# First pieces of a decoder layer in three transfers, and the last LayerNorm's mean from row sums of the last weights

## The chip, the cores and the metric

The kernel runs on one NeuronCore of a Trainium2 chip. The metric is the device time of one execution in microseconds. The times of several executions are given as a median with the lowest and the highest; one more execution was taken by the hardware profiler, and its trace is what the views below show. TensorE (PE) multiplies, VectorE (DVE), ScalarE (ACT) and GpSimd (POOL) work on elements, SyncE (SP) issues most of the transfers.

## The reference

One decoder layer for one sequence of 256 tokens, width 1024, all in float32:

```python
proj  = x @ w_in                      # [q | k | v | B | C | h | gate_attn | gate_conv]
y_att = attention(rope(q), rope(k), v) @ w_attn_out      # 8 heads of 64, causal
y_cnv = (B * causal_dwconv3(C * h)) @ w_conv_out
mix   = (sigmoid(g_att + b) * y_att + sigmoid(g_cnv + b) * y_cnv) @ w_o
x     = layer_norm(alpha * x + mix, ln1_g, ln1_b)
u     = causal_dwconv3(x @ w_up)                         # 2 x 2816 columns
f     = (silu(u_gate) * u_val) @ w_down                  # 2816 -> 1024
x     = layer_norm(alpha * x + f, ln2_g, ln2_b)          # eps 1e-5
```

`alpha` is 2 to the power 1/4. The last line, over rows of 1024, is the part whose end is changed.

## The kernel before, in words

Every product is made in three matmuls: an operand a is split into a high part (a copy rounded by the type fp32r) and a low part (a minus the high part), and high x high, high x low and low x high are added in PSUM. ScalarE makes the high part (`split_h`, L192, or `hl_split`, L219), VectorE the low part (`split_l`, L197, or L220). So each weight passes once through ScalarE and once through VectorE before TensorE reads it.

The weights (and x transposed) lie packed in device memory as chunks of up to 128 x 2048 numbers. `issue_dma` sends one chunk at a time on SyncE's queue into one of three `raw` buffers; `PIECES` says where a chunk is cut into several transfers. Chunk k of the first eight holds 128 rows of x transposed (256 columns), then those rows of the weights of q (512), k (512) and v (512).

The head of the program: the pieces of chunk 0 and 1 are issued; `warm_up` runs small matmuls on a tile `zeros` that VectorE has just set; VectorE casts x's first piece (L574) and makes its low part (L575), casts q's weights (L577) and makes their low part (L579); TensorE then runs q's passes on chunk 0 (`qkv_passes`, L568: pass 0 is high x high, pass 2 uses the low part of x, pass 1 the low part of the weights), and k's and v's behind it as their pieces land (ScalarE casts those, L219). Chunks 1 to 7 follow in a loop. Afterwards come convolution, gates and attention products, the mixing product, the first norm and the feed-forward part, in an order written out by hand; `slot` splits each weight unit a few units ahead of its use.

In the feed-forward part the 22 row blocks `f_tile(i)` of the hidden activations are made one after another and multiplied with the rows of `w_down` (`down`, `mm3`, L305 to L307) into four PSUM banks `dacc[t][nh]`: t is the block of 128 tokens, nh the half of 512 columns. The last `TAIL` = 8 rows of blocks are done for token block 0 first, then for token block 1 in three parts: half 0 of the columns with all eight (24 matmuls of 512), then columns 512 to 768 (`e2`) and columns 768 to 1024 (`e3`), 24 matmuls of 256 each (`down_part`). While TensorE does block 1, VectorE and GpSimd finish block 0: `residual` (L779, L781: alpha times x plus the bank, and `bn_stats`), `norm_stats` (L757 `bn_aggr` on VectorE, L758 the power -0.5 on GpSimd), `norm_apply` (L762 and L763 on VectorE for each half), and the output transfers.

Block 1's end, `finish(1)`: the residuals of the first three quarters are added as they come; behind the last matmul stand L1012 (add e3), L1013 (`bn_stats`), L757, L769 (subtract the mean and multiply by the gain, two halves), L758 beside it, and L766 (multiply by the power and add the bias) in pieces of 640 and 384 columns, each followed by its output transfer (on SyncE's and on ScalarE's queue).

Of the kernel before, what the change touches and what calls it, by code (L numbers as in the profile page):

```python
# [8 lines left out]
F32 = mybir.dt.float32  # L9
F32R = mybir.dt.float32r  # L10
# [3 lines left out]
ALU = mybir.AluOpType  # L14
# [123 lines left out]
def layer_kernel(ctx: ExitStack, tc: tile.TileContext, x, wpack, cpack, ln1_g, ln1_b, ln2_g, ln2_b, out):  # L138
# [11 lines left out]
    def acc_bank(name):  # L150
        return psum.tile([P, 512], F32, tag="acc", name=name)
# [4 lines left out]
    def scratch(shape, name, bufs=None, tag="scr"):  # L156
        return tmp.tile(shape, F32, tag=tag, name=name, bufs=bufs or 6)
# [11 lines left out]
    def issue_dma(c):  # L169
        while len(raws) <= c and len(raws) < len(chunks):  # L170
# [5 lines left out]
            if i == XR_CHUNK:  # L176
                nc.sync.dma_start(xr, x[0].rearrange("(t p) d -> p t d", p=P))

    def alloc(u, part, tag):
        k, n = units[u]["shape"]  # L180
        units[u][part] = wp.tile([P, k, n], F32R, tag=tag, name=f"{tag}{u}", bufs=HL_BUFS)
# [6 lines left out]
    def split_h(u):  # L188

        issue_dma(units[u]["chunk"] + RAW_BUFS - 1)  # L190
        alloc(u, "h", "wh")
        nc.scalar.activation(units[u]["h"], raw_of(u), AF.Copy)  # L192

    def split_l(u):

# [28 lines left out]
    nc.vector.memset(zeros, 0.0)  # L224
# [5 lines left out]
    warm = ps_bank("warm")  # L230

    def warm_up(n):
        for i in range(n):
            nc.tensor.matmul(warm[:, 0:P], zeros, zeros, start=True, stop=True)

    warm_up(36)

    mask = cst.tile([P, 384], F32, name="mask")
    nc.gpsimd.memset(mask, 0.0)
# [6 lines left out]
    neghalf = cst.tile([P, 1], F32, name="neghalf")  # L246
    nc.gpsimd.memset(neghalf, -0.5)
    neghalf2 = cst.tile([P, 1], F32, name="neghalf2")
    invf = cst.tile([P, 8], F32, name="invf")
    for i, f in enumerate(INV_FREQ):  # L250
        nc.gpsimd.memset(invf[:, i:i + 1], f)
# [312 lines left out]
    def qkv_passes(k, m, ts, ps):  # L564
        wh, wl = qkv_weights(k, m)
        for t in ts:
            for p in ps:
                nc.tensor.matmul(banks[m][t], (xl if p == 2 else xh)[:, k, t * P:(t + 1) * P], wl if p == 1 else wh,  # L568
                                 start=k == 0 and p == 0, stop=k == KT - 1 and p == 2)
# [1 line left out]

    split_start(1)
    issue_dma(RAW_BUFS - 1)
    nc.vector.tensor_copy(xh[:, 0, :], raws[0][:, 0:S])  # L574
    nc.vector.tensor_tensor(xl[:, 0, :], raws[0][:, 0:S], xh[:, 0, :].bitcast(F32), op=ALU.subtract)  # L575
    w0, wh0, wl0 = raw_of(1), units[1]["h"], units[1]["l"]
    nc.vector.tensor_copy(wh0[:, 0], w0[:, 0])  # L577
    qkv_passes(0, 0, (0, 1), (0, 2))
    nc.vector.tensor_tensor(wl0[:, 0], w0[:, 0], wh0[:, 0].bitcast(F32), op=ALU.subtract)  # L579
    qkv_passes(0, 0, (0, 1), (1,))  # L580
    split_part(1, 1, 2)
# [116 lines left out]
    def ps_pair(name):  # L698
        return pairs.tile([P, 2, 512], F32, tag="pair", name=name)
# [54 lines left out]
    def norm_stats(r, stats, pieces):  # L754

        mv = tmp.tile([P, 4], F32, tag="mv", name="mv", bufs=4)
        nc.vector.bn_aggr(mv[:, 0:2], stats[:, 0:pieces, :])  # L757
        nc.gpsimd.tensor_tensor(mv[:, 3:4], mv[:, 1:2], neghalf, op=ALU.pow)  # L758
        return mv

    def norm_apply(o, r, mv, g, b):
        nc.vector.scalar_tensor_tensor(o, r, mv[:, 0:1], g, op0=ALU.subtract, op1=ALU.mult)  # L762
        nc.vector.scalar_tensor_tensor(o, o, mv[:, 3:4], b, op0=ALU.mult, op1=ALU.add)  # L763

    def norm_second(r, mv, ln, cs):
        nc.vector.scalar_tensor_tensor(r[:, cs], r[:, cs], mv[:, 3:4], ln[:, 1, cs], op0=ALU.mult, op1=ALU.add)  # L766

    def norm_first(r, mv, ln, cs):
        nc.vector.scalar_tensor_tensor(r[:, cs], r[:, cs], mv[:, 0:1], ln[:, 0, cs], op0=ALU.subtract, op1=ALU.mult)  # L769
# [8 lines left out]
    def residual(t, nh, bank, res, r, stats, piece, c0, c1):  # L778
        nc.vector.scalar_tensor_tensor(r[:, c0:c1], res[:, t, c0:c1], ALPHA, bank[:, c0 - nh * 512:c1 - nh * 512],  # L779
                                       op0=ALU.mult, op1=ALU.add)  # L780
        nc.vector.bn_stats(stats[:, piece, :], r[:, c0:c1])  # L781
        if piece == 0:
            with_eps(stats)
# [19 lines left out]
        residual(0, nh, banks[nh], xr, r1[0], st1[0], nh, nh * 512, nh * 512 + 512)  # L803
    norm1(0, r1[0], st1[0])
    nc.scalar.activation(neghalf2, neghalf, AF.Silu)
    banks = [acc_bank(f"o1{nh}") for nh in range(2)]
    for k in range(4):
        wo_rows(k, 1, banks)
# [106 lines left out]
    def down(i, ts=(0, 1), nhs=(0, 1)):  # L915
        un = units[U[("dn", i // 2)] + i % 2]
        ft = f_tile(i)
        for t in ts:
            for nh in nhs:
                mm3(dacc[t][nh], ft[:, 0, t * P:(t + 1) * P], ft[:, 1, t * P:(t + 1) * P],  # L920
                    un["h"][:, 0, nh * 512:(nh + 1) * 512], un["l"][:, 0, nh * 512:(nh + 1) * 512],
                    i == 0, i == NP - 1 or (t == 1 and nh == 1 and i == NP - TAIL - 1))

    def down_part(i, bank, c):
        un = units[U[("dn", i // 2)] + i % 2]
        ft = f_tile(i)
        mm3(bank[:, 0:256], ft[:, 0, P:2 * P], ft[:, 1, P:2 * P],
            un["h"][:, 0, c * 256:(c + 1) * 256], un["l"][:, 0, c * 256:(c + 1) * 256], i == NP - TAIL, i == NP - 1)
# [4 lines left out]
    def take(n):  # L933
        out = []
        for stage, i in list(pending):
            if len(out) < n and i not in [p for _, p in out]:
                out.append((stage, i))
                pending.remove((stage, i))
        return out
# [49 lines left out]
        slot(k, stages)  # L989


    def finish(t):
        r = x1[:, t]
        stats = tmp.tile([P, 4, 6], F32, tag="stats", name=f"rstats{t}", bufs=2)
        if t == 0:
            for k in range(TAIL):
                down(NP - TAIL + k, (t,))
                slot(tail_from + k, take(2))
            assert not pending
            for nh in range(2):  # L1000
                residual(t, nh, dacc[t][nh], x1, r, stats, nh, nh * 512, nh * 512 + 512)
        else:
            for i in range(NP - TAIL, NP):
                down(i, (t,), (0,))
            nc.vector.scalar_tensor_tensor(r[:, 512:1024], x1[:, t, 512:1024], ALPHA, dacc[t][1], op0=ALU.mult, op1=ALU.add)
            for c in range(2):
                residual(t, 0, dacc[t][0], x1, r, stats, c, c * 256, c * 256 + 256)
            for c in range(2, 4):
                bank = ps_pair(f"e{c}")[:, 0]
                for i in range(NP - TAIL, NP):  # L1010
                    down_part(i, bank, c)
                nc.vector.tensor_tensor(r[:, c * 256:c * 256 + 256], r[:, c * 256:c * 256 + 256], bank[:, 0:256], op=ALU.add)  # L1012
                nc.vector.bn_stats(stats[:, c, :], r[:, c * 256:c * 256 + 256])  # L1013
        mv = norm_stats(r, stats, 2 if t == 0 else 4)
        if t == 0:
            for c in range(2):
                cc = slice(c * 512, (c + 1) * 512)
                norm_apply(r[:, cc], r[:, cc], mv, ln2[:, 0, cc], ln2[:, 1, cc])
                nc.sync.dma_start(out[0, t * P:(t + 1) * P, cc], r[:, cc])
            return  # L1020
        for c in range(2):
            norm_first(r, mv, ln2, slice(c * 512, c * 512 + 512))
        for cc, queue in ((slice(0, 640), nc.sync), (slice(640, D), nc.scalar)):
            norm_second(r, mv, ln2, cc)
            queue.dma_start(out[0, t * P:(t + 1) * P, cc], r[:, cc])

    for t in range(2):
        finish(t)


_INS = ['x', 'ln1_g', 'ln1_b', 'ln2_g', 'ln2_b']
# [39 lines left out]
```

## Time and profile before

| what | value |
|---|---|
| median of 3 runs | 365.47 us (365.17 to 365.59) |
| the profiled execution | 366.63 us |
| its span in the trace | 364.6 us |
| granted TensorE clock, mean | 0.997 |
| TensorE busy | 355.4 us |
| VectorE, ScalarE, GpSimd busy | 297.5, 226.3, 16.6 us |

The span runs from the first to the last recorded instruction; the profiled execution's time holds 2.03 us around it. In the rows of a timeline the first number is the start and the second the duration in us, then engine, source line, operation, the tile written and the tiles read, and how many instructions were merged; in square brackets stands how long the engine had been idle before and what ended that. Line numbers are those of the kernel before.

### The profile page before, as it was taken

Reading aid. Unit: us, or ns where it says so; the run is one execution under the profiler, and the core shown is the slowest. Engines: PE = TensorE matmul, PEld = TensorE weight load, DVE = VectorE, ACT = ScalarE, POOL = GpSimd, SP = SyncE. Lnnn points to the kernel's source line nnn. Section 1 sums busy time; section 2 is a strip of 40 time slices with the busy share of each in tenths; the row PEclk is TensorE's granted clock in tenths of the full one; section 3 lists DMA queues with packets and bytes.
Section 4 is the critical chain, followed back from the end, with each engine's and each line's share of the span. In section 5 each row is a group of like instructions: output and inputs, shape, how many; then the busy total and the mean of one; then the engine's idle time right before and its main releaser. Section 6 shows DMA issues by size and latency. Waiting matters only on the chain.

```text
span 364.6 us, 5227 instructions
## 1 busy us (share of the span) xinstructions
PE 355.4 (97%) x1956; PEld 306.8 (84%) x1956; DVE 297.5 (82%) x514; ACT 226.3 (62%) x392; POOL 16.6 (5%) x38
## 2 busy tenths in 40 slices
PE   8999999999999999999999999999999999999991
PEld 6788888888898888888888888888888888888891
DVE  4787888779795979989769789987968696999884
ACT  3575876577977966653457566765747476777400
POOL 2000000000000113301100000000000000000000
PEclk9999999999999999999999999999999999999998
DMA  8979565435654453787161835548281735653011
GB/s 259 325 254 338 220 236 184 156 115 201 262 192 150 138 214 134 238 320 299 49 231 39 303 124 229 173 172 309 63 322 53 293 108 239 232 230 117 2 58 58
DMA packets 11241, 69.62 MB, mean 191 GB/s; under 512 B 1232, under 2 KB 1616, under 8 KB 4176
## 3 DMA queue, kind: packets, MB, share of 16 engines
q1 hardware_dynamic: 10496, 67.00, 50.3%
q0 software_dynamic: 576, 2.10, 1.7%
q8 instruction: 15, 0.25, 0.3%
q10 hardware_dynamic: 144, 0.20, 0.1%
q14 instruction: 10, 0.08, 0.1%
HBM read 68.24 MB, written 1.05 MB: 190 GB/s over the span
## 4 chain that ended last, share of the span: by engine, by line
PE 96%; DMA 1%; DVE 1%; SPq 0%; ACT 0%; DVEq 0%; issue 0%
PE pb L323 20%; PE pb L330 10%; PE g L323 8%; PE d L305 5%; PE d L306 5%; PE d L307 5%; PE g L330 4%; PE y L323 4%; PE v L568 3%; PE q L568 3%; PE k L568 3%; PE b L323 2%; PE y L330 2%; PE c L323 2%; PE o L305 2%; PE o L307 2%
## 5 line engine op out<-in xcount | busy, mean ns | idle before, releaser
L197 DVE TENSOR_TENSOR wl<-raw,wh 128x1024 fp32r<-128x1024 f32 x99 | 121.0, 1225 | 25.3 <-ACT wh L192 25.1
L192 ACT ACTIVATE wh<-raw 128x1024 fp32r<-128x1024 f32 x99 | 103.7, 1054 | 32.2 <-DMA raw<-in_wpack 32.2
L323 PE MATMUL pb<-x1T,wh 128*128 128x512 f32 x320 | 76.2, 390 | 0.0
L323 PEld LDWEIGHTS pb<-x1T,wh 128*128 128x128 f32 x320 | 59.7, 188 | 12.1
L330 PEld LDWEIGHTS pb<-x1T,wl 128*128 128x128 f32 x320 | 41.0, 191 | 1.6
L330 PE MATMUL pb<-x1T,wl 128*128 128x256 f32 x320 | 41.5, 283 | 0.0
L220 DVE TENSOR_TENSOR wl<-raw,wh 128x1024 fp32r<-128x1024 f32 (+1 forms) x29 | 27.3, 981 | 7.5 <-ACT wh L219 7.3
L323 PE MATMUL g<-xT,wh 128*128 128x512 f32 x128 | 31.7, 395 | 0.0
L305 PE MATMUL d<-wh,f 128*128 128x512 f32 x80 | 31.3, 391 | 0.0
L306 PE MATMUL d<-wl,f 128*128 128x512 f32 x80 | 31.3, 391 | 0.0
L307 PE MATMUL d<-wh,f 128*128 128x512 f32 x80 | 31.1, 389 | 0.0
L219 ACT ACTIVATE wh<-raw 128x1024 fp32r<-128x1024 f32 (+1 forms) x29 | 23.7, 859 | 11.6 <-DMA raw<-in_wpack 7.5
L323 PEld LDWEIGHTS g<-xT,wh 128*128 128x128 f32 x128 | 23.2, 188 | 4.6
L857 DVE SCALAR_TENSOR_TENSOR fc<-fb,consts,fc 128x254 f32<-128x254 f32 x40 | 19.3, 483 | 1.4
L855 DVE SCALAR_TENSOR_TENSOR fc<-fb,consts,fc 128x255 f32<-128x255 f32 x40 | 19.1, 477 | 0.0
L849 ACT ACTIVATE fc<-fb,consts 128x256 f32<-128x256 f32 x40 | 18.0, 497 | 1.4 <-DVE fb L843 1.4
L307 PEld LDWEIGHTS d<-wh,f 128*128 128x128 f32 x80 | 15.0, 188 | 3.2
L305 PEld LDWEIGHTS d<-wh,f 128*128 128x128 f32 x80 | 15.1, 188 | 2.7
L839 ACT ACTIVATE fb<-pb 128x512 f32<-128x512 f32 x20 | 11.8, 592 | 8.7 <-PE pb L330 8.7
L306 PEld LDWEIGHTS d<-wl,f 128*128 128x128 f32 x80 | 15.1, 188 | 2.6
L330 PEld LDWEIGHTS g<-xT,wl 128*128 128x128 f32 x128 | 16.4, 191 | 0.7
L330 PE MATMUL g<-xT,wl 128*128 128x256 f32 x128 | 16.6, 282 | 0.0
(183 smaller groups left out, 580.1 us busy)
## 6 DMA issues: line engine op xcount, KB each, us to landing
raw<-in_wpack SPq DMA_DIRECT2D x55, 1024.0 KB, 5.0
raw<-in_wpack SPq DMA_DIRECT2D x6, 896.0 KB, 6.7
xr<-in_x SPq DMA_DIRECT2D x1, 1024.0 KB, 7.1
ln<-in_ln_g POOLq DMA_DIRECT2D x2, 512.0 KB, 5.7
ln<-in_ln_b POOLq DMA_DIRECT2D x2, 512.0 KB, 6.3
raw<-in_wpack SPq DMA_DIRECT2D x3, 256.0 KB, 3.3
raw<-in_wpack SPq DMA_DIRECT2D x1, 512.0 KB, 6.5
out<-x SPq DMA_DIRECT2D x2, 256.0 KB, 2.0
```

The lines of the kernel that those rows point to most:

```text
L192: nc.scalar.activation(units[u]["h"], raw_of(u), AF.Copy)
L197: nc.vector.tensor_tensor(units[u]["l"], raw_of(u), units[u]["h"].bitcast(F32), op=ALU.subtract)
L219: nc.scalar.activation(h, src, AF.Copy)
L220: (eng or nc.vector).tensor_tensor(l, src, h.bitcast(F32), op=ALU.subtract)
L305: nc.tensor.matmul(o, ah, bh, start=start, stop=False)
L306: nc.tensor.matmul(o, ah, bl, start=False, stop=False)
L307: nc.tensor.matmul(o, al, bh, start=False, stop=stop)
L323: nc.tensor.matmul(bank, un["h"][:, k, n0:n0 + P], b[:, k].rearrange("p a s -> p (a s)"), start=k == 0, stop=False)
L330: nc.tensor.matmul(bank[:, 0:S], un["l"][:, k, n0:n0 + P], b[:, k, 0], start=False, stop=k == nk - 1)
L568: nc.tensor.matmul(banks[m][t], (xl if p == 2 else xh)[:, k, t * P:(t + 1) * P], wl if p == 1 else wh, start=k == 0 and p == 0, stop=k == ...
L855: nc.vector.scalar_tensor_tensor(c[:, 1:S], pb[:, a * S:a * S + S - 1], w_ffn(1, j), c[:, 1:S], op0=ALU.mult, op1=ALU.add)
L857: nc.vector.scalar_tensor_tensor(c[:, 2:S], pb[:, a * S:a * S + S - 2], w_ffn(0, j), c[:, 2:S], op0=ALU.mult, op1=ALU.add)
```

## The change

Four edits:

1. Chunk 0 comes in three transfers instead of four: x's piece and q's weights together (768 columns), then k's, then v's. ScalarE casts x's piece, while VectorE casts q's weights; VectorE then makes the low part of x and the low part of q's weights. q's passes go over both token blocks with pass 0 first, then pass 2.
2. The warm-up matmuls read a constant of ones that the program's prologue sets, so the tile `zeros` and its memset go; there are 33 of them instead of 36.
3. For the last eight units of `w_down`, ScalarE also sums each row over columns 768 to 1024 (a copy with an accumulator) into `rowsum`. With these, the sum over the last 256 columns of block 1's product is known from the activations alone: ScalarE scales the eight blocks `f` by their row sums (`fs`), GpSimd adds the eight with one another (two additions of 512 columns, then 512, 256 and 128), ScalarE and VectorE split the result (`fsr`), and two matmuls with a moving operand of two columns of ones put the sums into a bank `mean`. They stand in TensorE's order behind the second of the eight blocks of `e3`.
4. Block 1's end no longer uses `bn_stats`. The sums of the first three quarters come as accumulator outputs of the residual additions; with `mean` they give the mean before the last quarter is there. ScalarE squares 768 columns with that mean as bias and accumulates; VectorE makes the first half of the norm for them. Behind the last matmul stand: the addition of `e3` (already less the mean), one multiply-and-sum over 256 columns, the power on GpSimd, beside it the first norm half of the last quarter, and the two pieces of 640 and 384 columns as before.

```diff
-PIECES = {0: (0, 256, 768, 1280, 1792), 1: (0, 768, 1792)}
+PIECES = {0: (0, 768, 1280, 1792), 1: (0, 768, 1792)}
...
         nc.scalar.activation(units[u]["h"], raw_of(u), AF.Copy)
+        if u in LAST_UNITS:
+            j = LAST_UNITS.index(u)
+            nc.scalar.activation(scratch([P, 256], f"rowsum{j}", tag="gs", bufs=3), raw_of(u)[:, 0, 768:1024], AF.Copy,
+                                 accum_out=rowsum[:, j:j + 1])
...
-    zeros = cst.tile([P, P], BF16, name="zeros")
-    nc.vector.memset(zeros, 0.0)
...
+        some = nc.const_aps.tensor(1.0, (P, P), BF16)
         for i in range(n):
-            nc.tensor.matmul(warm[:, 0:P], zeros, zeros, start=True, stop=True)
-    warm_up(36)
+            nc.tensor.matmul(warm[:, 0:P], some, some, start=True, stop=True)
+    warm_up(33)
...
-    nc.vector.tensor_copy(xh[:, 0, :], raws[0][:, 0:S])
+    w0, wh0, wl0 = raw_of(1), units[1]["h"], units[1]["l"]
+    nc.scalar.activation(xh[:, 0, :], raws[0][:, 0:S], AF.Copy)
+    nc.vector.tensor_copy(wh0[:, 0], w0[:, 0])
     nc.vector.tensor_tensor(xl[:, 0, :], raws[0][:, 0:S], xh[:, 0, :].bitcast(F32), op=ALU.subtract)
-    w0, wh0, wl0 = raw_of(1), units[1]["h"], units[1]["l"]
-    nc.vector.tensor_copy(wh0[:, 0], w0[:, 0])
-    qkv_passes(0, 0, (0, 1), (0, 2))
+    for p in (0, 2):
+        qkv_passes(0, 0, (0, 1), (p,))
...
+    for j in range(TAIL):
+        nc.scalar.activation(fs[:, j], f_tile(NP - TAIL + j)[:, :, P:2 * P].bitcast(F32), AF.Copy, scale=rowsum[:, j:j + 1])
+    fs_add(fs[:, 0:2], fs[:, 4:6])
+    fs_add(fs[:, 2:4], fs[:, 6:8])
...
+    fs_add(fs[:, 0:2], fs[:, 2:4])
+    fs_add(fs[:, 0], fs[:, 1])
+    fs_add(fs[:, 0, 0], fs[:, 0, 1])
...
+    for i in range(NP - TAIL, NP):
+        down(i, (1,), (0,))
+    for c in (1, 2, 0):
+        bank = dacc[1][1][:, 256 * c - 256:256 * c] if c else dacc[1][0]
+        nc.vector.scalar_tensor_tensor(part[c], x1[:, 1, cols3[c]], ALPHA, bank, op0=ALU.mult, op1=ALU.add,
+                                       accum_out=None if c == 1 else sums[:, c:c + 1])
+    hl_split(fsr[:, 0], fsr[:, 1], fs[:, 0, 0])
...
+    nc.vector.scalar_tensor_tensor(part[1], bank[:, 0:256], 1.0, part[1], op0=ALU.mult, op1=ALU.add, accum_out=sums[:, 1:2])
+    nc.vector.tensor_reduce(sums[:, 3:4], sums[:, 0:3], axis=mybir.AxisListType.X, op=ALU.add)
...
+    for i in range(NP - TAIL, NP):
+        down_part(i, bank, 3)
+        if i == NP - TAIL + 1:
+            for part_hl in range(2):
+                nc.tensor.matmul(mean[:, 0:2], fsr[:, part_hl], ones, start=part_hl == 0, stop=part_hl == 1)
+    for c, f in ((4, -1.0 / D), (5, -1.0 / (32 * D))):
+        nc.vector.tensor_scalar(sums[:, c:c + 1], mean[:, 0:1], sums[:, 3:4], f, op0=ALU.add, op1=ALU.mult)
+    for c in range(2):
+        nc.scalar.activation(scratch([P, 512], f"sq{c}")[:, 0:cols3[c].stop - cols3[c].start], part[c], AF.Square,
+                             bias=sums[:, 5:6], scale=1.0 / 32, accum_out=sums[:, 6 + c:7 + c])
+        nc.vector.scalar_tensor_tensor(res[:, cols3[c]], part[c], sums[:, 4:5], ln2[:, 0, cols3[c]], op0=ALU.add, op1=ALU.mult)
+    nc.vector.tensor_scalar(part[2], part[2], sums[:, 4:5], None, op0=ALU.add)
+    nc.vector.tensor_scalar(sums[:, 8:9], sums[:, 6:7], sums[:, 7:8], EPS, op0=ALU.add, op1=ALU.add)
+    nc.vector.tensor_tensor(part[2], part[2], bank[:, 0:256], op=ALU.add)
+    nc.vector.tensor_tensor_reduce(out=scratch([P, 256], "sq2"), in0=part[2], in1=part[2], scale=1.0 / D, scalar=sums[:, 8:9],
+                                   op0=ALU.mult, op1=ALU.add, accum_out=sums[:, 9:10])
+    nc.gpsimd.tensor_tensor(sums[:, 10:11], sums[:, 9:10], neghalf, op=ALU.pow)
+    nc.vector.scalar_tensor_tensor(res[:, cols3[2]], part[2], 1.0, ln2[:, 0, cols3[2]], op0=ALU.mult, op1=ALU.mult)
+    for cc, queue in ((slice(0, 640), nc.sync), (slice(640, D), nc.scalar)):
+        nc.vector.scalar_tensor_tensor(res[:, cc], res[:, cc], sums[:, 10:11], ln2[:, 1, cc], op0=ALU.mult, op1=ALU.add)
+        queue.dma_start(out[0, P:2 * P, cc], res[:, cc])
```

Two columns of ones are set by GpSimd at the start and copied by ScalarE to `ones` around the first norm. The rest of the program is unchanged, the order of the weights and their transfers too.

More of the change, by code (lines that the diff above doesn't have):

```diff
@@ L805, in layer_kernel @@
     nc.scalar.activation(neghalf2, neghalf, AF.Silu)
+    nc.scalar.activation(ones, ones32, AF.Copy)
     banks = [acc_bank(f"o1{nh}") for nh in range(2)]
@@ L989, in layer_kernel @@
         slot(k, stages)
[L992 to L1025, printed above, removed]
@@ L1027, in layer_kernel, with fs_add @@
-    for t in range(2):
-        finish(t)
+    for k in range(TAIL):
+        down(NP - TAIL + k, (0,))
+        slot(tail_from + k, take(2))
+    assert not pending
+    fs = big.tile([P, TAIL, 2, P], F32, tag="d8", name="fs")
+    for j in range(TAIL):
+        nc.scalar.activation(fs[:, j], f_tile(NP - TAIL + j)[:, :, P:2 * P].bitcast(F32), AF.Copy, scale=rowsum[:, j:j + 1])
+    def fs_add(a, b):
+        nc.gpsimd.tensor_tensor(a, a, b, op=ALU.add)
+    fs_add(fs[:, 0:2], fs[:, 4:6])
+    fs_add(fs[:, 2:4], fs[:, 6:8])
@@ new lines, in layer_kernel @@
+    r0 = x1[:, 0]
+    stats = tmp.tile([P, 4, 6], F32, tag="stats", name="rstats", bufs=2)
+    for nh in range(2):
+        residual(0, nh, dacc[0][nh], x1, r0, stats, nh, nh * 512, nh * 512 + 512)
+    mv = norm_stats(r0, stats, 2)
+    fs_add(fs[:, 0:2], fs[:, 2:4])
+    fs_add(fs[:, 0], fs[:, 1])
+    fs_add(fs[:, 0, 0], fs[:, 0, 1])
+    for c in range(2):
+        cc = slice(c * 512, (c + 1) * 512)
+        norm_apply(r0[:, cc], r0[:, cc], mv, ln2[:, 0, cc], ln2[:, 1, cc])
+        nc.sync.dma_start(out[0, 0:P, cc], r0[:, cc])
```

20 lines of the change are left out of this document (16 added, 4 removed).

## The prediction

> **What bounds the kernel now.** I read the page first: its span, the engines' busy shares and the chain that ended last.
>
> ```profile
> span 364.6 us, 5227 instructions
> PE 355.4 (97%) x1956; PEld 306.8 (84%) x1956; DVE 297.5 (82%) x514; ACT 226.3 (62%) x392; POOL 16.6 (5%) x38
> PE 96%; DMA 1%; DVE 1%; SPq 0%; ACT 0%; DVEq 0%; issue 0%
> ```
>
> TensorE is the chain for 96% of the span, so an edit elsewhere pays only where TensorE waits: before its first real matmul, and behind its last one. The change touches these two ends and puts work beside the stretch between. The chain of waits of the first 20 us, then the timeline of the first 14 us, show the head.
>
> ```profile
> 2.12 5.06 DMA raw<-in_wpack
> 7.88 1.92 PE v L568 x6
> 9.80 1.59 PE q L568 x6
> 11.39 1.38 PE k L568 x6
> ```
>
> ```profile
> 0.74 2.76 SPq L175 DMA_DIRECT2D raw<-in_wpack  x6
> 0.99 3.44 PE L234 MATMUL warm<-zeros 128*128 128x128 bf16 x36 [0.99 <-DVE zeros L224]
> 2.83 0.29 DVE L574 CAST xT<-raw 128x256 fp32r<-128x256 f32 x1 [1.89 <-DMA raw<-in_wpack]
> 3.16 0.42 DVE L575 TENSOR_TENSOR xT<-raw,xT 128x256 fp32r<-128x256 f32 x1
> 4.04 0.43 DVE L577 CAST wh<-raw 128x512 fp32r<-128x512 f32 x1 [0.46 <-DMA raw<-in_wpack]
> 4.50 0.69 DVE L579 TENSOR_TENSOR wl<-raw,wh 128x512 fp32r<-128x512 f32 x1
> 4.53 1.19 PE L568 MATMUL q<-wh,xT 128*128 128x512 f32 x4
> 4.97 0.63 ACT L219 ACTIVATE wh<-raw 128x512 fp32r<-128x512 f32 x1 [2.95 <-DMA raw<-in_wpack]
> 7.88 0.74 PE L568 MATMUL v<-wh,xT 128*128 128x512 f32 x2 [0.29 <-ACT wh L219]
> 8.22 0.42 ACT L219 ACTIVATE xT<-raw 128x256 fp32r<-128x256 f32 x1 [0.39 <-DMA raw<-in_wpack]
> ```
>
> x lands at about 2.8, q's weights at 4.0, k's at 4.95; the first real matmul starts at 4.53, right behind the cast of q's weights. v's piece, issued at 2.12, takes 5.06 us and lands at 7.18: it alone stops TensorE again, 0.29 us at 7.88. The undisturbed passes take 1.36 to 1.38 us (k at 11.39), v's took 1.92 and the next q 1.59. So the head loses time in two places, the start at 4.53 and some 1.1 us (0.29, 0.55, 0.22) that come from v's late landing.
>
> The end of the timeline shows the other wait.
>
> ```profile
> 350.65 0.39 PE L307 MATMUL d<-wh,f 128*128 128x512 f32 x1
> 351.16 0.68 DVE L1005 SCALAR_TENSOR_TENSOR x<-x,d 128x512 f32<-128x512 f32 x1
> 356.51 0.28 PE L307 MATMUL e<-wh,f 128*128 128x256 f32 x1
> 356.82 0.42 DVE L1012 TENSOR_TENSOR x<-x,e 128x256 f32<-128x256 f32 x1 [1.99 <-PE e L307]
> 357.28 0.43 DVE L1013 BATCH_NORM_STATS2 rstats<-x 128x6 f32<-128x256 f32 x1
> 357.74 0.26 DVE L757 BATCH_NORM_AGGREGATE mv<-rstats 128x2 f32<-128x24 f32 x1
> 358.04 1.44 DVE L769 SCALAR_TENSOR_TENSOR x<-x,mv,ln 128x512 f32<-128x512 f32 x2
> 358.08 0.55 POOL L758 TENSOR_TENSOR mv<-mv,neghalf 128x1 f32<-128x1 f32 x1 [9.33 <-DVE mv L757]
> 359.58 1.41 DVE L766 SCALAR_TENSOR_TENSOR x<-x,mv,ln 128x640 f32<-128x640 f32 x2
> ```
>
> Behind the last matmul come add, statistics, mean and variance and the first half of the norm: 2.76 us from 356.82 to 359.58, before the second half (L766) that feeds the output transfers. The second half and the transfers stay as they are.
>
> **The head, part by part.** One issue goes: six issues took 2.76 us, 0.46 each, so k's, v's and all later pieces are issued 0.46 earlier. x and q's weights now land together, 384 KB. The bounds of that landing are the x row (2.8) and the q row (4.0); the same bytes in half as many packets speak for less than 4.0, and three times x's bytes for more than 2.8. I take 3.45. Then ScalarE (0.42, as in the 8.22 row) and VectorE (0.43) cast x and q's weights side by side, where VectorE did both one after the other, and the first matmul can start at 3.45+0.48 = 3.93. The warm-ups no longer wait for a memset on VectorE; the constant is ready before any engine starts, so they begin with the first issue, near 0.77 instead of 0.99.
>
> ```profile
> 3.00:3.50 0.50, 0.50 (x7) 0.50 (x6) 0.47 (x2) 0.00 (x0) 0.00 (x0) 1.00 1.02 389
> 3.50:4.00 0.50, 0.50 (x11) 0.50 (x9) 0.08 (x1) 0.00 (x0) 0.00 (x0) 1.00 1.11 303
> ```
>
> (Windows: length, then TensorE's busy time and the number of its matmuls in the stretch; the granted clock is the 1.00 before the DMA share.) 36 warm-ups took 3.44 us, 0.096 each; 33 take 3.15 and end at 3.92. The pace quickens after 3.5 (11 rows against 7), and an earlier start spends more of them at the slow pace, so I take 4.0. The first real matmul then starts at 4.0 instead of 4.53: 0.5 us. The Trainium skill's "TensorE: Matmul & The Clock Gate" (Part 1) says that the faster pace comes with a free-running activity window, which shifts by up to 0.5 us from run to run; by it the warm-ups could end near 4.3 and leave 0.2 of the 0.5. No second run here shows the shift.
>
> This start counts only if v's wait shrinks with it. v's piece is issued 0.46 earlier. If it lands 0.46 earlier too, everything behind moves by about 0.5: head gain 0.5, the value that I take. If its landing is set by the bytes ahead of it, it stays at 7.18 and the head gains nothing. If it lands as quickly after its issue as k's did (4.95 less 1.66, 3.3 us), at 1.66+3.3 = 5.0, the 1.1 us of starvation go as well: gain 1.4 to 1.6. Ends 0 and 1.5. q's low half (wl) is one place that gets worse: VectorE makes it after the 0.43 cast and xl's 0.42, ready 1.6 after the landing at 5.05, where four matmuls from 4.0 end at 4.92; that 0.1 is inside the 0.5, since k and v behind it had such gaps as well.
>
> **Beside the last weights.** Eight sums of weight rows go to ScalarE behind eight splits.
>
> ```profile
> 321.00:341.50 20.50, 20.50 (x114) 17.90 (x113) 20.22 (x35) 15.55 (x27) 0.00 (x0) 1.00 0.40 153
> L413 ACT ACTIVATION_READ_ACCUMULATOR sm<-sm,st 128x1 f32 x16 | 3.0, 186 | 0.0
> ```
>
> Columns: TensorE, its weight loads, VectorE, ScalarE. Each sum is a copy of 256 columns (0.42) plus a read of the accumulator (0.19): 8 x 0.61 = 4.9 us against 20.50-15.55 = 4.95 us of idle ScalarE. It fits barely, but starts overlap and the idle pieces stand just before instructions that wait for VectorE, so I cost it at nothing; without that cover it is 0.3 to 0.8 us. The eight products behind them (ScalarE idle from 342) and the two large additions on GpSimd end by 347, under TensorE's matmuls.
>
> **The chain that makes the mean.** GpSimd then raises block 0's variance to the power, and only after that adds 512, 256 and 128 columns; ScalarE and VectorE split the result; two tiny matmuls stand in TensorE's queue behind the sixth matmul of the last quarter, with 18 real ones queued behind them. The 48 quarter matmuls go from 350.88 to 356.51, 0.12 each, so the slot is at 350.88+30x0.12 = 354.48. Rows for the chain:
>
> ```profile
> 348.21 0.55 POOL L758 TENSOR_TENSOR mv<-mv,neghalf 128x1 f32<-128x1 f32 x1 [172.72 <-DVE mv L757]
> 349.04 0.75 DVE L763 SCALAR_TENSOR_TENSOR x<-x,mv,ln 128x512 f32<-128x512 f32 x1
> L458 POOL TENSOR_TENSOR ac<-ac 128x256 f32<-128x256 f32 x4 | 3.2, 803 | 116.5 <-ACT ac L457 116.5
> L197 DVE TENSOR_TENSOR wl<-raw,wh 128x1024 fp32r<-128x1024 f32 x99 | 121.0, 1225 | 25.3 <-ACT wh L192 25.1
> 153.18 0.78 POOL L715 TENSOR_TENSOR m<-m 128x256 f32<-128x256 f32 x1 [0.80 <-DVE m L714]
> 153.28 1.76 DVE L197 TENSOR_TENSOR wl<-raw,wh 128x1024 fp32r<-128x1024 f32 x1
> 174.31 0.75 DVE L762 SCALAR_TENSOR_TENSOR x<-xr,mv,ln 128x512 f32<-128x512 f32 x1
> 174.36 1.12 POOL L758 TENSOR_TENSOR mv<-mv,neghalf 128x1 f32<-128x1 f32 x1 [9.34 <-DVE mv L757]
> ```
>
> 256 columns take 0.80; 512 lie between 0.80 and 1.60, I take 1.3; 128 between 0.40 and 0.80, I take 0.5. Alone: 348.76+1.3+0.8+0.5 = 351.4, and the split by 352.1: 2.4 us early. But the last four rows show the two engines excluding each other: a VectorE subtraction of two SBUF tiles that began 0.10 after a GpSimd addition took 1.76 instead of 1.22, until the addition was over; the power at 174.36, begun 0.05 after VectorE's, took 1.12 instead of 0.55. Block 0's norm (four L762/L763 of 0.75, from 348.16) reads two SBUF tiles, so it and the additions take turns: 348.8+1.3+0.75+0.8+0.75+0.5+0.75 = 353.65, less some 0.7 for overlapped hand-overs, 352.95 where the norm ended at 351.24 before. Then VectorE has three residual additions (0.68 and twice 0.42, 1.35 with overlaps) and the low half of the split (0.2): 354.5, and the tiny matmuls start at 354.55 to 354.7. I take 0.15 of stall; ends 0 and 1.0. The Trainium skill's "SBUF — State Buffer" (SBUF: two separate sides) states this as an exclusive lock on a shared port pair, held for a whole instruction by whoever starts first; the trace agrees with the 1.76. It speaks against this change, which puts long GpSimd additions beside VectorE's norm.
>
> The two matmuls cost 0.12 each by the quarter's pace, 0.24 (ends 0.05 and 0.5). TensorE so ends 0.39 later relative to its start.
>
> **Behind the last matmul.** Now stand: the addition (0.46 to the next start), a multiply-and-sum over 256 columns, its accumulator read, the power, and L766's counterpart.
>
> ```profile
> L402 DVE CUSTOM_DVE_ANT_0 sm<-s,mask 128x256 f32<-128x256 f32 x8 | 3.1, 419 | 0.0
> L402 DVE DVE_READ_ACCUMULATOR2_ANT st<- 128x1 f32 x16 | 1.3, 83 | 0.0
> ```
>
> 0.46+0.42+0.08, 0.08 to GpSimd (357.74+0.26 to 358.08), 0.55 and 0.04 back: 1.63. A 256-column multiply of two SBUF tiles starts on VectorE just ahead of the power and holds it back as at 174.36; at half of 0.75 less the hand-over that is 0.25: 1.88 against 2.76, gain 0.88 (ends 0.5 and 1.15). The mean, the first norm halves and the squares of the other 768 columns run during the last 18 matmuls: VectorE has about 354.6 to 356.9 for a sum over e's third quarter (0.43), two small ones, 0.75, 0.4, 0.4 and 0.15, and is ready at 356.9, just before TensorE's end at 357.2. What is late next, if this slips, is that row of VectorE work.
>
> **The sum.** Head 0.5, tail 0.88-0.24-0.15 = 0.5: 1.0 us less. On the profiled execution, 366.63 us (2.03 around the span), that is 365.6; it lies 1.16 above the median of 365.47, on which I put it: 364.5.
>
> **Rivals.**
> (1) The engines do not get in each other's way here: no stall (0.15) and no held-back power (0.25), tail 0.9, total 1.4: 364.1. For it: the power at 348.21, 0.05 behind VectorE's, took only 0.55. Against: the 1.76.
> (2) v's late landing does not come back; head 1.5, total 2.0: 363.5. For it: k's 3.3 us against v's 5.06; against: more pieces were queued behind v.
> (3) v's landing stays at 7.18: head 0, total 0.5: 365.0.
> (4) Slower: the row-sum chain comes so late that TensorE waits at the tiny matmuls. If each addition takes twice its row, as the power did (1.12 against 0.55), and waits for VectorE's norm: 348.8+2.6+1.6+1.0+three times 0.75 and the split's 0.4 is 356.65, a stall of 2.2; less 1.15 of the rest (0.5+0.88-0.24), 1.05 us slower: 366.5. It decides from 1.15 us of stall, additions of some 1.6 times their rows. Against: eight L715 and four L458 rows stand near 0.8 beside a busy VectorE.
> (5) The warm-ups or the landing eat the start and VectorE's late norm the end: 365.5, no change.
>
> **Chances.** This measurement tells 0.2%, 0.73 us, from no change: faster means below 364.74. Forecast 0.47 (own range 364.0 to 365.0, of which 0.32 faster), (1) 0.17, (2) 0.13, (3) 0.10, (4) 0.09, (5) 0.04. Faster 0.32+0.17+0.13 = 0.62; slower 0.09 and a rounding for unseen mishaps of its kind, 0.10; within 0.2% the rest, 0.28. The range takes in (2) at 363.5 and (3) at 365.0 with 0.2 above it, and leaves out (4).
>
> **What would show it.** In the profile after: first q matmul at 4.0, v's first at 7.4, one cast of x on ScalarE; L763's counterpart of block 0 starting near 350 instead of 349.04; the tiny matmuls without idle of over 0.3 ahead of them; 1.9 us from the last addition's start to the 640-column row. It is wrong if v starts at 7.9 again, if TensorE idles at the tiny matmuls, or if the last addition waits for VectorE and not TensorE.

## The result, and the profile after

The changed kernel takes 364.84 us (median of 18 runs, 364.02 to 366.01); the kernel before, beside it, 366.07 us (18 runs, 365.17 to 366.52). The ratio is 0.9967 with an interval of 0.9959 to 0.9976: 1.2 us less, where 0.97 was forecast. The profiled execution took 365.12 us, 1.51 less than the 366.63 of before. One execution of all that follow, in `two_again`, ran in a slower state (445.72 us at a granted clock of 0.753) and is left out of the ratios.

The page of the changed kernel, its span, busy times and chain:

```profile
span 363.3 us, 5272 instructions
PE 355.9 (98%) x1955; PEld 308.5 (85%) x1955; DVE 298.5 (82%) x518; ACT 234.7 (65%) x423; POOL 22.5 (6%) x44
PE 95%; issue 2%; DVE 1%; POOL 1%; POOLq 0%; DVEq 0%
```

TensorE is still the chain, for 95% of the span. ScalarE and GpSimd are 8.4 and 5.9 us busier, the row sums and the additions, and none of it lengthens the span.

The head, by its chain of waits (start, length, what):

```profile
0.78 3.68 PE warm L241 x33
4.46 2.48 PE q L578 x6
6.94 1.39 PE k L578 x6
8.33 1.37 PE v L578 x6
9.70 1.36 PE q L578 x6
11.06 1.36 PE k L578 x6
```

and by its timeline (start, length, instruction, what ended the idle time before it):

```profile
3.78 0.42 ACT L585 ACTIVATE xT<-raw 128x256 fp32r<-128x256 f32 x1 [1.76 <-DMA raw<-in_wpack]
3.78 0.43 DVE L586 CAST wh<-raw 128x512 fp32r<-128x512 f32 x1 [3.78 <-DMA raw<-in_wpack]
4.35 2.05 PE L578 MATMUL q<-wh,xT 128*128 128x512 f32 x4
4.61 0.63 ACT L227 ACTIVATE wh<-raw 128x512 fp32r<-128x512 f32 x1 [0.41 <-DMA raw<-in_wpack]
6.25 0.63 ACT L227 ACTIVATE wh<-raw 128x512 fp32r<-128x512 f32 x1 [1.02 <-DMA raw<-in_wpack]
```

x and q's weights land together at 3.78 and are cast side by side; v's weights land at 6.25 instead of 7.2, and v never waits. But q's first four matmuls take 2.05 us where they took 1.19: TensorE's pace had not yet doubled. So v's first matmul stands at 8.17, later than the 7.88 of before, although nothing holds it up but the matmuls ahead of it. The second chunk's k starts at 11.06 instead of 11.39, so this execution's head gains 0.33 us.

The middle, by windows (TensorE, its weight loads, VectorE, ScalarE) and by the timeline:

```profile
321.00:341.50 20.50, 20.50 (x115) 17.90 (x114) 20.00 (x35) 17.47 (x42) 0.00 (x0) 1.00 0.37 145
```

```profile
348.37 3.38 POOL L1011 TENSOR_TENSOR fs<-fs 128x512 f32<-128x512 f32 x3
348.68 1.60 DVE L774 SCALAR_TENSOR_TENSOR x<-x,mv,ln 128x512 f32<-128x512 f32 x1
350.21 1.22 DVE L773 SCALAR_TENSOR_TENSOR x<-x,mv,ln 128x512 f32<-128x512 f32 x1
351.46 0.83 DVE L774 SCALAR_TENSOR_TENSOR x<-x,mv,ln 128x512 f32<-128x512 f32 x1
353.50 0.28 DVE L228 TENSOR_TENSOR fsr<-fs,fsr 128x128 fp32r<-128x128 f32 x1
354.11 0.28 PE L1052 MATMUL mean<-ones,fsr 128*128 128x2 f32 x2
```

VectorE's norm rows of 0.75 us have become 1.60, 1.22 and 0.83 beside GpSimd's three additions; the low half (L228) is ready 0.33 us before the tiny matmuls (L1052), and these show no idle time ahead of them.

The end:

```profile
356.38 0.28 PE L317 MATMUL e<-wh,f 128*128 128x256 f32 x1
356.69 0.42 DVE L1063 TENSOR_TENSOR part<-part,e 128x256 f32<-128x256 f32 x1 [0.33 <-PE e L317]
357.15 0.48 DVE L1064 CUSTOM_DVE_ANT_0 sq<-part,sums 128x256 f32<-128x256 f32 x1
357.73 0.67 POOL L1066 TENSOR_TENSOR sums<-sums,neghalf 128x1 f32<-128x1 f32 x1 [5.97 <-DVE sums L1064]
358.43 1.41 DVE L1069 SCALAR_TENSOR_TENSOR res<-res,sums,ln 128x640 f32<-128x640 f32 x2 [0.44 <-POOL sums L1066]
```

From the last matmul's start to the 640-column row it is now 2.05 us (358.43 less 356.38) instead of 3.07 (359.58 less 356.51): 1.02 gained, less 0.23 for the two tiny matmuls (from the first to the last quarter matmul it is 5.86 us instead of 5.63), 0.80 in all. Head 0.33 and tail 0.80 put the 640-column row 1.15 earlier. The execution is 1.51 shorter: 0.36 lies behind that row and outside the span, where nothing was predicted.

### The profile page after: what moved, and what is told of

Read it like the earlier page. It is cut to its first block, busy times and chain, and to the rows that moved or that the text cites. A ratio compares the mean times of both kernels' runs of the same rounds, so it can differ in the third digit from the quotient of the medians.

```text
span 363.3 us, 5272 instructions
## 1 busy us (share of the span) xinstructions
PE 355.9 (98%) x1955; PEld 308.5 (85%) x1955; DVE 298.5 (82%) x518; ACT 234.7 (65%) x423; POOL 22.5 (6%) x44
## 4 chain that ended last, share of the span: by engine, by line
PE 95%; issue 2%; DVE 1%; POOL 1%; POOLq 0%; DVEq 0%
PE pb L333 20%; PE pb L340 11%; PE g L333 8%; PE d L315 4%; PE d L316 4%; PE d L317 4%; PE g L340 4%; PE y L333 4%; PE q L578 3%; PE k L578 3%; PE v L578 3%; PE b L333 2%; PE y L340 2%; PE c L333 2%; PE o L315 2%; PE h L333 2%
## 5 line engine op out<-in xcount | busy, mean ns | idle before, releaser
L228 DVE TENSOR_TENSOR wl<-raw,wh 128x1024 fp32r<-128x1024 f32 (+1 forms) x29 | 27.3, 983 | 7.3 <-ACT wh L227 7.1
```

## Experiments

### The two halves of the change apart

`h_only` is the kernel before with the changed head (three transfers, casts side by side, 33 warm-ups on the constant); `t_only` the changed kernel with the old head; `pieces` and `warm` split the head once more.

```diff
 # pieces, against before (warm-ups as before)
-PIECES = {0: (0, 256, 768, 1280, 1792), 1: (0, 768, 1792)}
+PIECES = {0: (0, 768, 1280, 1792), 1: (0, 768, 1792)}
...
-    nc.vector.tensor_copy(xh[:, 0, :], raws[0][:, 0:S])
...
+    nc.scalar.activation(xh[:, 0, :], raws[0][:, 0:S], AF.Copy)
...
 # warm, against before
...
+        some = nc.const_aps.tensor(1.0, (P, P), BF16)
...
-            nc.tensor.matmul(warm[:, 0:P], zeros, zeros, start=True, stop=True)
+            nc.tensor.matmul(warm[:, 0:P], some, some, start=True, stop=True)
-    warm_up(36)
+    warm_up(33)
```

The dots stand for lines left out here: `pieces` has the order of casts and of q's passes of the change as well, and `warm` has no tile `zeros`.

> The head's two edits alone (three transfers with the casts side by side, 33 warm-ups on the constant), the end as before. Theory: head and end are independent terms, the head is worth 0.3 to 0.5 us of the 1.2 measured: ratio to before 0.9986 to 0.9992. Rival: the head gives nothing on the median, because TensorE's clock is still slow when the first real matmuls start (the first four q matmuls took 2.05 us in the profile after against 1.19 before): ratio 0.9995 to 1.0005. In its trace the late rise of the clock, if it comes from the phase of a window and not from the edit, can come at any time from 3.5 to 6.5 us.

> The end's edits alone (row sums, mean ahead of the last quarter), the head as before. Theory: 0.8 us of the 1.2 come from here, as in the profile after: last quarter matmul to the 640-column row 2.04 us against 3.07 before, 0.23 paid for the two tiny matmuls, no stall ahead of them: ratio 0.9976 to 0.9980. Rival: the whole gain is here and the head gives nothing: 0.9965 to 0.9970.

> Of the head only the three transfers and the casts side by side; 36 warm-ups on the memset tile as before. Theory: v's landing near 6.2 instead of 7.18 carries the head's gain, so this alone gives what both edits of the head give: ratio equal to that of the head alone within 0.0005, v's first matmul without idle ahead of it. Rival: the earlier warm-ups are needed to use the earlier landing, and this alone gives nothing.

> Of the head only the warm-ups: 33 on the constant, which start near 0.78 instead of 0.99; four transfers as before. Theory: the first real matmul still waits for q's weights at 4.0 to 4.5, so nothing: ratio 0.9995 to 1.0005. Rival: fewer warm-ups end before the clock rises and the first real matmuls run at the slow pace more often: up to 0.5 us slower, ratio up to 1.0014.

Measured, as ratios to before on the same chip: `h_only` 0.9970 (0.9956 to 0.9984), `t_only` 0.9985 (0.9970 to 0.9999), `pieces` 0.9977 (0.9961 to 0.9992), `warm` 0.9999 (0.9985 to 1.0013). What the changed head gains comes with the three transfers: `pieces` differs from `h_only` by less than either interval, and the earlier and fewer warm-ups alone are worth nothing that can be measured. But `h_only` gains more than either expectation gave it, and `t_only` less. The tail alone gives 0.57 us less in the medians, although its trace has the whole 0.80 between the matmuls and the 640-column row (last matmul 355.98, row 358.02). Both differences are found behind that row. This is what SyncE and GpSimd do at the program's end, in the closing line of before, of `pieces`, of `t_only` and of the changed kernel, in this order (instruction, count, durations in ns, first and last start in us):

```profile
L1067 SPq EVENT_SEMAPHORE  x10: 17/28/28, 363.2 to 364.5; - x10
L1067 SPq DRAIN  x3: 7/7/7, 363.7 to 364.0; - x3
L1067 PEldq DRAIN  x2: 13/1179/2345, 354.5 to 364.1; - x2
L1067 POOLq EVENT_SEMAPHORE_RANGE_CLEAR  x1: 139/139/139, 364.1 to 364.1; - x1
```

```profile
L1068 SPq EVENT_SEMAPHORE  x10: 17/28/28, 360.2 to 363.4; - x10
L1068 SPq DRAIN  x3: 7/7/7, 362.6 to 362.9; - x3
```

```profile
L1109 SPq EVENT_SEMAPHORE  x10: 17/28/28, 361.7 to 363.3; - x10
L1109 SPq DRAIN  x3: 7/7/7, 362.2 to 362.5; - x3
L1109 PEldq DRAIN  x2: 13/1220/2428, 353.9 to 362.5; - x2
L1109 POOLq EVENT_SEMAPHORE_RANGE_CLEAR  x1: 139/139/139, 362.9 to 362.9; - x1
```

```profile
L1109 SPq EVENT_SEMAPHORE  x10: 17/28/28, 359.7 to 363.3; - x10
L1109 SPq DRAIN  x3: 7/7/7, 362.1 to 362.4; - x3
L1109 PEldq DRAIN  x2: 13/1222/2430, 354.3 to 362.5; - x2
L1109 POOLq EVENT_SEMAPHORE_RANGE_CLEAR  x1: 139/139/139, 362.9 to 362.9; - x1
```

SyncE waits there for the transfers' semaphores one after the other, in the order of their numbers, 0.06 us each once they are there. Which transfer has which number follows from how many were issued before it. In before and `t_only` the last output transfer has the first number: SyncE stands at the first wait until 3.6 us behind the 640-column row (363.2 less 359.58), then goes through the others, and drains at 4.1. With one transfer fewer at the head, the numbers move by one and the last output transfers come last in the row: in `pieces` and the changed kernel the first waits pass 1.3 us behind the row (360.2 less 358.91 and 359.7 less 358.43), and the drain comes at 3.7. That is 0.43 us which one transfer fewer at the start saves at the very end. Against it stands a pause that came with the tail: GpSimd clears the semaphores directly behind TensorE's drain in before (364.1 and 364.1), but 0.4 us behind it in `t_only` and the changed kernel (362.5, then 362.9). From the 640-column row to the span's end it is 4.97 us in before, 4.53 in `pieces` and `h_only`, 5.33 in `t_only` and 4.91 in the changed kernel, and where the same head and tail were run again each value came back within 0.02 us (`warm` 4.97, the second profile of the changed kernel 4.91, without warm-ups 4.89).

Outside the span, the kernels with the changed tail take less as well: the time less the span is 2.02 us in before (mean of 34 executions, 1.77 to 2.20), 2.03 in `warm`, 2.01 in `pieces` and 1.91 in `h_only`, but 1.78 in `t_only` (12 executions, 1.73 to 1.83) and 1.79 in the changed kernel. No trace reaches there.

Taking the part from the first quarter matmul to the span's end, as each kernel's one trace has it, out of its median span leaves the head:

| kernel | median span | first quarter matmul to end | rest | before on the same chip, rest | head gain |
|---|---|---|---|---|---|
| `h_only` | 363.3 | 13.24 | 350.06 | 350.62 | 0.56 |
| `pieces` | 363.4 | 13.24 | 350.16 | 350.62 | 0.46 |
| `warm` | 364.3 | 13.68 | 350.62 | 350.62 | 0.00 |
| `t_only` | 363.95 | 13.23 | 350.72 | 350.62 | -0.10 |
| changed | 363.05 | 12.82 | 350.23 | 350.36 | 0.13 |
| changed, again | 363.2 | 12.82 | 350.38 | 350.62 | 0.24 |

The four kernels with the new head gain 0.13 to 0.56, 0.35 in the mean, each known to 0.3 to 0.5 us either way, as its ratio is. Three kernels of a later section that have the new head, too, give by the same reckoning 0.25 (`late1`), 0.32 (`late2`) and 0.32 (`no_adds`).

### The warm-ups taken away

```diff
-    warm_up(33)
+    warm_up(0)
```

> The changed kernel without any warm-up matmul. Theory A, the warm-ups earn by starting the clock's rise early: the first q matmul can start at the cast's end, near 4.0 to 4.1, but TensorE runs at half pace for some 2.7 to 5.5 us from there, so q and k take 2.5 us each instead of 1.4 and v about 2: 1.5 to 2.5 us slower than the changed kernel, ratio to before 1.001 to 1.004. Theory B, the rise is late anyway (as in the changed kernel's profile, at 6.2) and the warm-ups only stand in q's way: first q at 4.1 instead of 4.35, time the same or 0.3 us less than the changed kernel's, ratio 0.996 to 0.997.

366.16 us, ratio 0.9993 (0.9985 to 1.0002): 1.0 us slower than the changed kernel's ratio gives. Theory A in its mechanism, but at a smaller price than its 1.5 to 2.5 us. The windows of its trace, and of a second profile of the changed kernel (`after_again`, below), show by the number of matmuls when the pace doubles:

```profile
9.00:10.00 1.00, 1.00 (x4) 0.76 (x4) 0.74 (x2) 0.74 (x2) 0.00 (x0) 1.00 1.03 423
10.00:11.00 1.00, 1.00 (x7) 0.79 (x6) 0.55 (x1) 0.00 (x0) 0.00 (x0) 1.00 1.16 358
```

```profile
3.00:4.00 1.00, 1.00 (x14) 0.92 (x12) 0.13 (x1) 0.14 (x1) 0.00 (x0) 1.00 1.08 393
```

```profile
6.00:7.00 1.00, 1.00 (x4) 0.78 (x4) 0.08 (x1) 0.63 (x1) 0.00 (x0) 1.00 1.01 396
7.00:8.00 1.00, 1.00 (x6) 0.81 (x5) 0.92 (x2) 0.77 (x2) 0.00 (x0) 1.00 1.09 418
```

Without warm-ups TensorE starts at 4.36 and speeds up only at 9.6, 5.2 us later. In the second profile of the changed kernel it speeds up at 3.5, 2.7 us after its first matmul; in the first profile (the last fence) between 6 and 7, some 5.6 us after it. The other traces lie between: 2.7 in before and `h_only`, 4.1 to 4.3 in `t_only` and `pieces`, 5.0 in `late1` and `no_adds`. So the doubling comes anywhere from 2.7 to 5.6 us after the first matmul, and what a late one costs is half the time for which q's and k's matmuls run before it. The granted clock in these rows is 1.00 throughout, and the count of matmuls tells it instead. The 1.00 ahead of the doubling is no measurement: each trace's record of the clock begins only there, at 3.67 us in before, 3.53 and 6.43 in the two profiles of the changed kernel and 9.60 without warm-ups.

### GpSimd's additions: later, much later, and gone

`late1`, `late2` and `late3` put one, two or three more additions of 512 columns between block 0's power and the last three. `no_adds` leaves the last three out (most of the sum over the eight blocks is then missing from block 1's mean).

```diff
     mv = norm_stats(r0, stats, 2)
+    for _ in range(1):          # 2 in late2, 3 in late3
+        fs_add(fs[:, 4:6], fs[:, 6:8])
     fs_add(fs[:, 0:2], fs[:, 2:4])
     fs_add(fs[:, 0], fs[:, 1])
     fs_add(fs[:, 0, 0], fs[:, 0, 1])
```

> The changed kernel with one more GpSimd addition of 512 columns (its result is not used) between block 0's power and the three last additions. Theory A, GpSimd and VectorE take turns at two-SBUF-input operations: the first half norm row waits for one more addition, block 0's norm ends about 0.9 us later than in the changed kernel (near 1.8 us after the power's end plus 2.7), the low half of the split is ready 0.9 later, and the two tiny matmuls, which had 0.2 to 0.3 us in hand, make TensorE wait 0.6 us (0.3 to 0.9): time 0.6 us above the changed kernel's, ratio to before 0.9985. Theory B, no turns: VectorE's norm rows stay as they are, the additions end 1.3 later, at about 353.1, the split is ready at 353.6 and no wait appears: ratio as the changed kernel's, 0.997.

> The same with three more GpSimd additions of 512 columns. This is the price of the slower rival: the additions end 3 x 1.3 = 3.9 us later, near 355.6, the split near 356.1, where the tiny matmuls' place in the queue is at 354.0: TensorE waits 2.1 us (1.7 to 2.8) at the tiny matmuls and the time rises by as much: 1.0 us above before (ratio 1.002 to 1.005). If instead the wait can be partly made up (the VectorE work behind the third quarter is done meanwhile, so nothing of it is late at the last matmul), the tail behind the last matmul is the same 2.0 us and the rise is still one for one; it is less only if the last 18 quarter matmuls run faster than 0.12 us each after the pause.

> The changed kernel without the three last GpSimd additions (it leaves out most of the sum over the eight blocks, so block 1's mean is not the right one). If the turns of GpSimd and VectorE are what lengthened VectorE's two first norm rows (1.60 and 1.22 us), all four are 0.75 again and the norm ends near 351.0 instead of 352.3. If this delay costs nothing on the path, as no wait at the tiny matmuls says, the time is the changed kernel's, ratio to before 0.997; if it does cost, up to 0.3 us less, 0.996.

> The changed kernel with two more GpSimd additions of 512 columns. From the kernel with three, whose GpSimd chain ended at 355.6 with the tiny matmuls' place at 353.7, one addition less (1.27 us) lets the chain end 1.27 earlier: TensorE waits 1.0 us (0.8 to 1.2) at the tiny matmuls. Theory A, the clock falls only behind a long pause such as the 2.28 us of the kernel with three additions: the granted clock stays 1.00 and the time is 1.0 us above the changed kernel's, ratio to before 0.9985 to 1.0005. Theory B, any pause of about 1 us brings the clock to 0.50 for the rest of the quarter matmuls: 2 us more, ratio 1.004 to 1.007.

`late1`: ratio 0.9975 (0.9965 to 0.9985), 0.3 us above the changed kernel's, with intervals that overlap; theory A by its trace:

```profile
348.76 1.60 DVE L774 SCALAR_TENSOR_TENSOR x<-x,mv,ln 128x512 f32<-128x512 f32 x1
350.28 1.77 DVE L773 SCALAR_TENSOR_TENSOR x<-x,mv,ln 128x512 f32<-128x512 f32 x1
352.09 1.11 DVE L774 SCALAR_TENSOR_TENSOR x<-x,mv,ln 128x512 f32<-128x512 f32 x1
354.74 0.27 PE L1054 MATMUL mean<-ones,fsr 128*128 128x2 f32 x1 [0.38 <-DVE fsr L228]
```

The second norm row waits for an addition of 512 instead of 256 columns and takes 1.77 instead of 1.22, and so on down to TensorE, which waits 0.38 us for the low half. From the first to the last quarter matmul it is 6.39 us instead of 5.86: 0.5.

`no_adds`: all four norm rows take 0.75 to 0.78 (the last starts at 350.47), so the additions are what lengthens them; ratio 0.9965 (0.9952 to 0.9978), the changed kernel's. The delay costs nothing on the path, and 0.3 us is all that it has in hand.

`late2`: TensorE waits 0.94 us at the tiny matmuls, as worked out, and needs 7.28 us from the first to the last quarter matmul, 1.4 more than the changed kernel; the granted clock stays 1.00. Ratio 1.0005 (0.9992 to 1.0018), at the upper end of theory A: the gain is gone.

`late3`: ratio 1.0064 (1.0040 to 1.0087), 2.3 us slower than before instead of 1.0. The wait has the length that was worked out, and then comes something else. First its timeline, then the windows (the granted clock is the third figure from the right):

```profile
356.01 0.70 PE L1054 MATMUL mean<-ones,fsr 128*128 128x2 f32 x2 [2.28 <-ACT fsr L227]
```

```profile
352.73:353.73 1.00, 1.00 (x9) 0.80 (x7) 1.00 (x3) 0.00 (x0) 1.00 (x1) 1.00 0.00 0
358.25:359.25 1.00, 1.00 (x6) 1.00 (x6) 0.56 (x3) 0.36 (x2) 0.00 (x0) 0.50 0.00 0
```

Behind the pause of 2.28 us the granted clock is 0.50, and the last 18 quarter matmuls take 0.21 us each instead of 0.12, until the end. Not in each of the seven runs: their mean granted clocks go from 0.984 to 0.996 and their times from 371.17 to 367.34; six are at 0.991 or below. The one at 0.996, a clock like that of the other kernels, is 0.9 us above before: about the price that the slower rival was given. No trace of that run was kept.

### One transfer fewer still

```diff
-PIECES = {0: (0, 768, 1280, 1792), 1: (0, 768, 1792)}
+PIECES = {0: (0, 768, 1792), 1: (0, 768, 1792)}
```

> The changed kernel with the first chunk in two transfers: x with q's weights, k's weights with v's (512 KB). Theory A, v's landing is set by its place among the pieces and by how many issues stand ahead of it: k's and v's weights land together near 5.5 (5.0 to 6.2), everything behind is issued another 0.46 earlier, k comes later than the 4.6 of the changed kernel but still ahead of its matmuls at 5.6 to 6.8, and v never stops TensorE: 0 to 0.5 us less than the changed kernel, ratio to before 0.995 to 0.997. Theory B, a landing of 512 KB takes to 6.5 or beyond, so that k's matmuls wait where q's run at full pace: the same or up to 0.7 us more than the changed kernel, ratio 0.997 to 0.999.

> The kernel with the first chunk in two transfers once more, beside the changed kernel. If the issue that is saved counts, it is 0.2 to 0.5 us below the changed kernel here as well; if the 0.25 us between the two in the runs so far (ratios 0.9960 and 0.9967, whose intervals overlap) is scatter, the two are within 0.2 us of each other.

> The changed kernel once more, beside the one with two transfers on the same chip. Ratio to before 0.9955 to 0.998. In its profile the start of the second chunk's matmuls differs from 9.54 by up to 0.9 us either way, set by the time at which TensorE's pace doubles and by v's landing; the tail is the same to 0.05 us: 2.04 us from the last quarter matmul's start to the 640-column row.

The first time 364.79 us, ratio 0.9960 (0.9945 to 0.9974); the second time 0.9965 (0.9951 to 0.9979), where the changed kernel beside it had 0.9962 (0.9948 to 0.9976). k's and v's weights land together at 5.52, k's matmuls then wait in pieces, and v does not. Part of each expectation comes true, and the two kernels are the same: no version here is faster than the changed one beyond the intervals. In the second profile of the changed kernel the second chunk starts at 8.70 instead of 9.54, 0.84 earlier by the pace and v's landing alone, and the tail is the same, 2.05 us. With two transfers the last output transfers stand one place further ahead in SyncE's row, at 4.97 instead of 4.91 from the 640-column row to the end.

## Why the prediction was right, point by point

- **The total.** 0.97 us was forecast and 1.2 measured, inside the forecast's own range. Its absolute 364.5 rested on a median of three runs of before, 365.47; 18 runs gave 366.07. That the sum fits so well is in part luck. The head was taken too large (0.5 for 0.13 to 0.35), the tail too small (0.5 for 0.80), and these two errors nearly cancel; 0.3 us came from the program's end, where nothing was forecast.
- **The signs.** One sign that the prediction named against itself appeared: v's first matmul was to start at 7.4, and "it is wrong if v starts at 7.9 again"; in the profile it starts at 8.17. What the sign was meant to tell, v's weights landing late again, did not happen (6.25, and no wait): q's matmuls ran at half pace until then. In the second profile v starts at 7.34. Nor does L763's counterpart start near 350; it starts at 348.68 and takes 1.60, so the turn is taken inside the row. The other signs came as named: no idle time at the tiny matmuls, 1.74 us where 1.9 stood, and a last addition that waits for TensorE.
- **The head, 0.5.** In the right place, and a little large: 0.33 in the profile, 0.35 in the mean of four kernels. Two of its terms were off. The landing of x with q's weights was taken at 3.45 and came at 3.5 to 3.9; cast and start took 0.57 instead of 0.48; so q's first matmul starts at 4.35, not at 4.0. And the warm-ups' pace was taken from one trace. That trace has one of the earliest doublings, at 2.7 us after the first matmul, and the changed kernel's has the latest. The Trainium skill's page "TensorE: Matmul & The Clock Gate" (Part 1) gives 0.5 us either way for the shift; the traces here show 2.9 us from the earliest to the latest, and the measurement decides. It is about the length of the window that the page names (an activity window of 3.4 us), and that fits its free running better than its 0.5.
- **v's landing.** "Lands 0.46 earlier" is not what the traces show: 5.7, 5.9 and 7.2 with four transfers, 5.4 to 7.1 with three. The 7.18 of before, and the 1.1 us of starvation with it, were one draw from this scatter. Rivals (2) and (3) were both priced from that draw; neither holds as a rule.
- **Row sums, 0.** Right: ScalarE's busy time in that window goes from 15.55 to 17.47 us of 20.50, each sum takes 0.40 and its read 0.19, and TensorE does not wait.
- **Additions and norm taking turns.** Right, and as `late1` and `no_adds` show, it is what lengthens the rows: 512, 256 and 128 columns were taken at 1.3, 0.8 and 0.5; alone, 512 take 1.27. The norm ends at 352.3 instead of 352.95, less the 0.36 by which everything came earlier here, so 0.3 better than forecast. The Trainium skill's "SBUF — State Buffer" (SBUF: two separate sides), with its exclusive lock for a whole instruction, agrees with the 1.60, the 1.77 of `late1` and the 0.75 of `no_adds`. Rival (1), no turns, is refuted as a mechanism, although its price for the tail, 0.9, lies nearer to the 0.80 measured than the forecast's 0.5.
- **Stall 0.15, tiny matmuls 0.24, gain behind the last matmul 0.88.** 0, 0.23 and 1.02 (2.05 us where 3.07 stood). Of the 1.88 us from the last addition's start, 1.74 came: the power was held back 0.11 to 0.12 (0.67 instead of 0.55) and not 0.25.
- **"The second half and the transfers stay as they are", and 2.03 around the span.** This is the step that failed, and its two parts nearly cancel within the trace: SyncE's waits 0.43 shorter, GpSimd's clear 0.37 later, and 0.25 less outside the span. Together 0.3 us in the change's favour, about as much as its head.
- **Rival (4), slower.** Its place and its threshold were right (`late2`, with 0.94 us of stall, is level with before), its price was not: behind a pause of 2.3 us the clock falls in six of seven runs, and the loss more than doubles (2.3 us instead of 1.0).

## What to carry to other kernels

A gain of a few tenths of a us at a program's start or end can come from places that the edit does not touch: count the transfers, see in which order the program's end waits for them, and compare the time from the last computing row to the span's end before believing a sum. One profile shows one draw of the landings and of the clock's rise; at this size the head's terms need several executions. Work that runs beside a matmul stream is free until its slack is used up, so measure the slack (here 0.3 us) by adding delay until the stream waits.

## What the runs showed of the hardware that was not expected

- TensorE's pace doubles 2.7 to 5.6 us after its first matmul, differently in each execution of the same kernel (2.7 and 5.6 in two profiles of the changed one), while the granted clock in the rows reads 1.00.
- A pause of 0.94 us left TensorE's granted clock at 1.00; one of 2.28 us brought it to 0.50 for the remaining 4.3 us, in six of seven runs by their mean clocks. Where between the two it begins was not tried; in that trace the clock fell 2.4 us after the start of the last matmul before the pause, and at the ends of the other traces 2.7 to 5.6 us after the last matmul's start.
- The order in which the program's end waits for its transfers is worth 0.43 us here, and one transfer fewer at the head moved it; with a second one fewer (`two`) 0.06 of it was lost again.
- GpSimd pauses some 0.4 us ahead of clearing the semaphores in the kernels with the changed tail, not in those with the old one. With one more addition the pause stands one GpSimd instruction earlier in the program's end, with two more two instructions earlier, with three fewer three instructions later, and it is as long in each (0.40 to 0.43 us); from the 640-column row to the end that gives 5.04, 4.93 and 4.90 us. With three more additions no pause is seen (4.55). So it keeps its place in the count of GpSimd's instructions. By what means is open, as is the cause of the 0.25 us outside the span.
